# A two-layer diffusion trunk: values, queries and keys first, attention in half-tile steps beside four projections, residual loaded per token tile, first modulation in f32 by quarters

## The chip, the cores and the metric

The kernel runs on the 8 cores of one Trainium2 chip. Each core works on its own 1536 tokens and there is no traffic between cores. The metric is the time of the slowest core in microseconds (us).

An execution can fall into a second, slower state: the cores of one die (0 to 3 or 4 to 7), sometimes of both, get a lower TensorE clock, and the time grows whatever the kernel. Only fast runs are compared here. Where one die was slow I read the cores of the other, undisturbed die, and say so.

Engines in the profile lines: PE is TensorE, PEld its weight loads, DVE VectorE, ACT ScalarE, POOL GpSimd.

## The reference, cut to what matters

```python
# per layer, D = 2048, 4 branches of width 512; context tokens and latent tokens have their own modulation
m = silu(cond) @ w_ada + b_ada                  # shift1, scale1, gate1, shift2, scale2, gate2
h = rmsnorm(x, norm1_g) * (1 + sc1) + sh1
q, k, v, u, vg, xf, xp, gl = split(h @ w_in)    # 7 x 512 columns, then 4 x 2048 gate columns
branches = (attention(rmsnorm(q), rmsnorm(k), v),        # 8 heads of 64, neighbourhood + cached keys
            gelu(u) * (W_s @ rmsnorm(gelu(vg)) + b_s),   # gated branch
            fourier_mix(xf), multiscale_pool(xp))
merged = sum_i sigmoid(gl_i + b_i) * (branches[i] @ w_branch[i])
x = x + g1 * (merged @ w_out)
h2 = rmsnorm(x, norm2_g) * (1 + sc2) + sh2
x = x + g2 * (relu(h2 @ w_mlp1)**2 @ w_mlp2)
```

## The kernel before

A Python builder emits all instructions in order, per engine, with semaphores from a dependency tracker. The tokens of a core are three tiles of 512 (tile 0 is context, 1 and 2 are latent). A projection group is 16 matmuls of 512 columns into one PSUM bank. Weights come through a ring of 7 slots, cast to bf16 by POOL-issued transfers. Work of other engines is placed with `defer(n, fn)`: `fn` is emitted n hooks later. A hook comes after each group. Attention works in steps, or chunks (scores, exponentials and value products for a block or two of keys); a unit is all the steps of one head pair and one token tile, two of them for context and nine for a latent tile.

```python
    def hook(self):
        cur, self.deferred = self.deferred, []
        for d in cur:
            d[0] -= 1
        ...                                   # those at 0 are emitted, then the side generators step

    def gelu2(self, b, out, wk, i):
        g1, g2 = self.G1[i % 2], self.G2[i % 2]
        ps = self.bank(b)
        self.act(g1.ap(), ps, AF.Square, self.pk(b), [g1.k()])
        self.ts(g1.ap(), g1.ap(), 0.044715, 1.0, ALU.mult, ALU.add, [g1.k()], [g1.k()])
        self.tt(g2.ap(), g1.ap(), ps, ALU.mult, [g1.k(), self.pk(b)], [g2.k()])
        ...                                   # tanh on ACT, last operation on DVE

    # mixers: vg, u, values (gated branch as side work), q/k, then
        self.use_banks([0, 1], [])
        at = self.side(self.attention(l, BR, QP, QRt, KRt, QC, KX, V, VC), 1.0)
        ...                                   # xf, xp, Fourier, pool beside it

    # attention, at the end of a unit (one head pair, one token tile):
                self.act(self.RD.ap(), self.bank(DB), AF.Ln, self.pk(DB), [self.RD.k()], scale=2048.0)
                self.act(self.RD.ap(), self.RD.ap(), AF.Exp, [self.RD.k()], [self.RD.k()], scale=-1.0)
                self.tt(BR.ap(tt, j), self.bank(OB), self.RD.ap(), ALU.mult, ...)
    # and its loop, one step after each projection group:
        for i in range(0, len(chunks), 2):
            cur = chunks[i:i + 2]
            ...
            for ch in cur:
                scores(ch)
            for ch in prev:
                pv(ch)
            for ch in cur:
                probs(ch)
            prev = cur
            yield

    def out_proj(self, l, MRG, X, nrm):
        ...                                   # loads the residual of all three tiles
        def tile(slot, oc, tt):
            b = self.group(slot, MRG, tt, range(NCH))
            i = 0 if tt == 0 else 1
            self.stt(X.ap(tt, oc), self.bank(b), self.mv(l, 2, oc, i), X.ap(tt, oc), ALU.mult, ALU.add, ...)
            nrm.stat(tt, oc, 1)               # square on ACT now, ones-matmul one hook later
```

At the start all 32 tiles of the first modulation go through the ring in bf16, and after the last of them the norm of all three token tiles follows.

Of the kernel before, what the change touches and what calls it, by code (L numbers as in the profile page):

```python
# [13 lines left out]
NCH = 16  # L14
# [181 lines left out]

class Slot:
# [4 lines left out]
class Ring:  # L202


    def __init__(self, b, plan):
        self.b, self.plan = b, plan
        self.n = 0
        self.free = list(range(RING))
        self.home = []
        self.specs = []  # L210
        self.regs = [Reg(b.nc, b.base, f"W{i}", RING_OFF + i * SLOT, SLOT, BF16) for i in range(RING)]
# [29 lines left out]
class Builder:  # L241
    def __init__(self, plan=None):
        nc = bass.Bass("TRN2", target_bir_lowering=False)
        self.nc = nc
        self.decl_dram()
        base = nc.alloc_sbuf_tensor("POOL", [128, USABLE // 4], F32)
        self.base = nc_addr(base)
        self.tr = Tracker(nc)
        self.plan = plan
        self.alloc()  # L250
        self.ring = Ring(self, plan)
        self.deferred = []
        self.sides = []



    def decl_dram(self):
# [19 lines left out]
        self.d_cb = di("cb", (128, 768), BF16)  # L277
# [13 lines left out]
    def alloc(self):  # L291
# [10 lines left out]
        self.CB = const("CB", 768, BF16)  # L302
# [9 lines left out]
        self.PERM, self.FCC = cb(384, 512), cb(512, 768)  # L312
# [12 lines left out]
        self.ROPE = sreg("ROPE", 0, 8 * k, F32)  # L325
        self.G1 = [sreg(f"G1{i}", 8 * k + 4 * k * i, 2 * k, F32) for i in range(2)]
        self.G2 = [sreg(f"G2{i}", 10 * k + 4 * k * i, 2 * k, F32) for i in range(2)]
        self.QF = [sreg(f"QF{i}", 16 * k + 2 * k * i, 2 * k, F32) for i in range(2)]
        self.QR = [sreg(f"QR{i}", 20 * k + 2 * k * i, 2 * k, F32) for i in range(2)]
        self.QT = sreg("QT", 24 * k, 2 * k, F32)  # L330
        self.QS = [sreg(f"QS{i}", 26 * k + k * i, k, BF16) for i in range(2)]
        self.TAB = sreg("TAB", 0, 11776, F32)
        self.P = [sreg(f"P{i}", 11776 + 2048 * i, 2048, BF16) for i in range(3)]
        self.RD = sreg("RD", 11776 + 6144, 2048, F32)
        self.KC = sreg("KC", 11776 + 8192, 4096, BF16)
        self.PM = sreg("PM", 24064, 3200, BF16)
        self.WPB = sreg("WPB", 24064 + 3200, 1024, BF16)
# [30 lines left out]
    def hook(self):  # L368
# [3 lines left out]
        for d in cur:  # L372
            if d[0] <= 0:
                d[1]()
            else:
                self.deferred.append(d)
        for s in list(self.sides):
# [69 lines left out]

    def group(self, slot, src, tt, cs, lo=0):
# [3 lines left out]
        self.mms([(self.bank(b), slot.ap[:, lo + j * 128:lo + (j + 1) * 128], src.ap(tt, c), j == 0, j == n - 1)  # L452
                  for j, c in enumerate(cs)], r=[slot.keys, src.ks(tt, cs)], w=self.pk(b))
# [66 lines left out]
    class Norm:  # L520
# [23 lines left out]
        def apply(self, tt):  # L544
            b, l = self.b, self.l
# [3 lines left out]
            b.rsqrt(R.ap(), b.bank(bk), b.pk(bk), [R.k()])  # L549
            i = 0 if tt == 0 else 1  # L550
            for c in range(NCH):
                t = self.tmp['t'][c % len(self.tmp['t'])]
                b.stt(t.ap(), self.X.ap(tt, c), b.mod(l, i, self.which, c), R.ap(), ALU.mult, ALU.mult,
                      [self.X.k(tt, c), R.k(), b.MOD.k()], [t.k()])
                b.act(self.H.ap(tt, c), t.ap(), AF.Identity, [t.k(), b.MV.k()], [self.H.k(tt, c)],
                      bias=b.mv(l, 0 if self.which == 0 else 3, c, i), scale=1.0)
# [10 lines left out]
    def token_major(self, l, which, H, consume):  # L567
        slots = [self.ring.get(lambda b, kq=kq: b.d_tm[l, which, kq]) for kq in range(4)]
        for n in range(12):
            tt, q = divmod(n, 4)  # L570
            b = self.dbank()
            self.mms([(self.bank(b), H.ap(tt, c, q * 128, q * 128 + 128),
                       slots[c // 4].ap[:, (c % 4) * 512:(c % 4 + 1) * 512], c == 0, c == 15) for c in range(NCH)],
                     r=[s.keys for s in slots] + [H.ks(tt, range(NCH))], w=self.pk(b))
# [17 lines left out]
    def gelu2(self, b, out, wk, i):  # L592

        g1, g2 = self.G1[i % 2], self.G2[i % 2]
        ps = self.bank(b)
        self.act(g1.ap(), ps, AF.Square, self.pk(b), [g1.k()])
        self.ts(g1.ap(), g1.ap(), 0.044715, 1.0, ALU.mult, ALU.add, [g1.k()], [g1.k()])
        self.tt(g2.ap(), g1.ap(), ps, ALU.mult, [g1.k(), self.pk(b)], [g2.k()])
        self.act(g1.ap(), g2.ap(), AF.Tanh, [g2.k()], [g1.k()], scale=0.7978845608028654)
        self.stt(out, g1.ap(), 1.0, ps, ALU.add, ALU.mult, [g1.k(), self.pk(b)], [wk])  # L600

    def mixers(self, l, H, BR, WK, regs):
        tr = self.tr
        self.use_banks([0, 1, 2, 3], [4, 5, 6, 7])
        nm = lambda s: f"{s}_{l}"
        hreg, breg, wreg = regs
        brbase = breg.off

        BSB = self.reg(nm("BSB"), brbase + 8 * KB, 2 * KB, F32)
        GRW = self.reg(nm("GRW"), brbase + 10 * KB, 2 * KB, F32)  # L610
        WSB = self.reg(nm("WSB"), brbase + 12 * KB, KB, BF16)
        SSQ = self.reg(nm("SSQ"), brbase + 13 * KB, KB, BF16)
        SS = self.reg(nm("SS"), brbase + 14 * KB, 64, F32)
        NVS = [self.reg(nm(f"NVS{i}"), brbase + 24 * KB + 2 * KB * i, 2 * KB, F32) for i in range(2)]
        NKS = [self.reg(nm(f"NKS{i}"), brbase + 28 * KB + 2 * KB * i, 2 * KB, F32) for i in range(2)]
        VGT = [self.reg(nm(f"VG{n}"), brbase + (n // 4) * 16 * KB + (n % 4) * KB, KB, BF16) for n in range(12)]
        wo = wreg.off
        pair = lambda n, j, off, nb: self.reg(nm(f"{n}{j}"), wo + j * 8 * KB + off, nb, BF16)
# [5 lines left out]
        V = [self.reg(nm(f"V{n}"), wo + 32 * KB + n * KB, KB, BF16) for n in range(12)]  # L624
        VC = [self.reg(nm(f"VC{n}"), wo + 44 * KB + n * KB, KB, BF16) for n in range(4)]

        tr.dma('sp', lambda e: e.dma_start(out=BSB.ap(), in_=bass.AP(self.d_bs.tensor, l * 512, [[0, 128], [1, 512]])),
               w=[BSB.k()])
        tr.dma('sp', lambda e: e.dma_start(out=GRW.ap(), in_=bass.AP(self.d_gn.tensor, l * 512, [[0, 128], [1, 512]])),
               w=[GRW.k()])  # L630
        tr.dma('pool', lambda e: e.dma_start(out=WSB.ap(), in_=self.d_ws[l]), w=[WSB.k()])


        def vg_done(n, b):
            self.gelu2(b, VGT[n].ap(), VGT[n].k(), n)
            tr.op('act', lambda e: e.activation(out=SSQ.ap(), in_=VGT[n].ap(), func=AF.Square,
                                                accum_out=SS.ap(n, n + 1)),
                  r=[VGT[n].k()], w=[SSQ.k(), SS.k()])
        self.tables('exp_and_others')
        self.token_major(l, 0, H, vg_done)  # L640

        cnt = [0]
        for oc in range(4):
            def u_done(tt, b, oc=oc):
                self.gelu2(b, BR.ap(tt, 4 + oc), BR.k(tt, 4 + oc), cnt[0])
                cnt[0] += 1
            self.feature_major(l, 8 + oc, H, u_done)

        def gmlp():
            self.tables('natural_log_exp_and_others')  # L650
            self.rsqrt(SS.ap(0, 12), SS.ap(0, 12), [SS.k()], [SS.k()], scale=1.0 / BW, four=1)
            yield
            for n in range(12):
                self.stt(VGT[n].ap(), VGT[n].ap(), SS.ap(n, n + 1), GRW.ap(), ALU.mult, ALU.mult,
                         [VGT[n].k(), SS.k(), GRW.k()], [VGT[n].k()])
                tt, q = divmod(n, 4)
                b = self.abank()
                self.mms([(self.bank(b, g * 128, g * 128 + 128), VGT[n].ap(g * 128, g * 128 + 128),
                           WSB.ap(g * 128, g * 128 + 128), True, True) for g in range(4)],
                         r=[VGT[n].k(), WSB.k()], w=self.pk(b))  # L660
                t = self.QF[n % 2]
                self.tt(t.ap(), self.bank(b), BSB.ap(), ALU.add, [self.pk(b), BSB.k()], [t.k()])
                r, o = BR.loc(tt, 4)
                u = r.ap(o, o + 4 * TT).rearrange("p (g t) -> p g t", g=4)[:, :, q * 128:q * 128 + 128]
                keys = [r.k(o + g * TT + q * 128, o + g * TT + q * 128 + 128) for g in range(4)]
                self.stt(u, t.ap().rearrange("p (g t) -> p g t", g=4), 0.5, u, ALU.mult, ALU.mult,
                         [t.k()] + keys, keys)
                yield
        gs = self.side(gmlp(), 1.0)
# [8 lines left out]
        self.token_major(l, 1, H, v_done)  # L678
# [697 lines left out]
```

## Time and profile before

Four fast runs took 6255.7 to 6257.9 us, median 6257.2. The stage lines are in the prediction below. In short, for layer 0 of the slowest core:

| stage | us | what PE does in it |
|---|---|---|
| first modulation and norm, up to the first projection | about 181 | waits for transfers, then for the norm |
| all mixers, up to the merge | 709 (end) | waits on small statistics, on the cached keys, on the norm |
| merge | 857 | full |
| output projection | 300 | waits about 100 us for squares |
| MLP | 1411 | full |

How to read it: where PE is busy throughout at clock 1.00, nothing was expected from moving work about. What can be had lies in the other stages.

### The profile page before, as it was taken

Reading aid. Unit: us, or ns where it says so; the run is one execution under the profiler, and the core shown is the slowest. Engines: PE = TensorE matmul, PEld = TensorE weight load, DVE = VectorE, ACT = ScalarE, POOL = GpSimd, SP = SyncE. Lnnn points to the kernel's source line nnn. Section 1 sums busy time; section 2 is a strip of 40 time slices with the busy share of each in tenths; the row PEclk is TensorE's granted clock in tenths of the full one; section 3 lists DMA queues with packets and bytes.
Section 4 is the critical chain, followed back from the end, with each engine's and each line's share of the span. In section 5 each row is a group of like instructions: output and inputs, shape, how many; then the busy total and the mean of one; then the engine's idle time right before and its main releaser. Section 6 shows DMA issues by size and latency. Waiting matters only on the chain.

```text
span 6256.2 us, 73139 instructions; the slowest of 8 cores (6228.0 to 6256.2 us)
## 1 busy us (share of the span) xinstructions
PE 5727.5 (92%) x27208; PEld 2520.0 (40%) x27208; DVE 1899.5 (30%) x2721; ACT 1187.8 (19%) x1831; POOL 384.6 (6%) x732
## 2 busy tenths in 40 slices
PE   2788899999669999999998889999986899999999
PEld 0333344444224444444443334444432344444444
DVE  0543222222123222233344332222221333333333
ACT  1544211111121000000043451111111300000000
POOL 1000000100000000000000000000000000000000
PEclk6999899999999999999999999999999999999999
DMA  9232355553315555555343213322241222222223
GB/s 201 58 64 61 65 95 98 101 98 60 103 31 88 96 90 98 91 101 98 51 123 66 56 56 58 53 51 51 51 121 24 44 51 51 51 51 51 52 53 109
DMA packets 118728, 464.72 MB, mean 74 GB/s; under 512 B 13296, under 2 KB 15088, under 8 KB 109424
## 3 DMA queue, kind: packets, MB, share of 16 engines
q0 software_dynamic: 104704, 376.49, 34.5%
q1 hardware_dynamic: 13680, 83.56, 3.8%
q8 instruction: 226, 3.70, 0.2%
q14 instruction: 118, 0.97, 0.1%
HBM read 798.16 MB, written 29.36 MB: 132 GB/s over the span
## 4 chain that ended last, share of the span: by engine, by line
PE 87%; ACT 4%; DMA 4%; DVE 3%; issue 2%; ACTq 0%; DVEq 0%; SPq 0%; POOLq 0%
PE PS L425 87%; DMA W_96<-w_ada 2%; DVE x_B L418 1%; DMA SEL<-sel 1%; ACT bf_C L403 1%; DMA x_B<-xin 0%; DMA x_B<-xres 0%; DMA KC<-ckT 0%; DVE x_C L418 0%; ACT bf_A L403 0%; DVE x_A L418 0%; ACT G_62 L403 0%; ACT n_sq_11991 L403 0%; ACT n_sq_34868 L403 0%; ACT n_sq_11992 L403 0%
## 5 line engine op out<-in xcount | busy, mean ns | idle before, releaser
L418 DVE SCALAR_TENSOR_TENSOR x_B<-PS,MV,x_B 128x512 f32<-128x512 f32 x432 | 324.4, 751 | 581.6 <-PE PS L425 558.1
L403 ACT ACTIVATE RL_59<-PS 128x512 f32<-128x512 f32 x192 | 114.7, 597 | 1734.7 <-PE PS L425 1734.7
L425 PE MATMUL PS<-bf_A,W_99 128*128 128x512 bf16 x1344 | 299.4, 382 | 1.3 <-DVE VG_1_24334 L418 0.7
L412 DVE TENSOR_TENSOR HID<-RL_59 128x512 bf16<-128x512 f32 x192 | 133.1, 693 | 548.4 <-ACT RL_59 L403 548.4
L412 DVE TENSOR_TENSOR HID<-RL_60 128x512 bf16<-128x512 f32 x192 | 133.0, 693 | 538.2 <-ACT RL_60 L403 538.2
L425 PE MATMUL PS<-bf_A,W_93 128*128 128x512 bf16 x1296 | 293.8, 386 | 1.9 <-DVE bf_A L412 1.9
L425 PE MATMUL PS<-bf_C,W_95 128*128 128x512 bf16 x1296 | 291.0, 383 | 1.3 <-DVE VG_0_941 L418 0.7
L425 PE MATMUL PS<-bf_A,W_97 128*128 128x512 bf16 x1248 | 275.4, 379 | 0.0
L425 PE MATMUL PS<-bf_A,W_95 128*128 128x512 bf16 x1200 | 265.1, 379 | 0.0
L425 PE MATMUL PS<-bf_A,W_98 128*128 128x512 bf16 x1200 | 264.7, 379 | 0.0
L418 DVE SCALAR_TENSOR_TENSOR x_C<-PS,MV,x_C 128x512 f32<-128x512 f32 x216 | 162.2, 751 | 320.7 <-PE PS L425 312.7
L418 DVE SCALAR_TENSOR_TENSOR x_A<-PS,MV,x_A 128x512 f32<-128x512 f32 x216 | 162.2, 751 | 306.6 <-PE PS L425 299.7
L425 PE MATMUL PS<-bf_C,W_97 128*128 128x512 bf16 x1152 | 254.6, 379 | 0.0
L425 PE MATMUL PS<-bf_C,W_96 128*128 128x512 bf16 x1056 | 239.9, 386 | 8.6 <-ACT bf_C L403 8.6
L425 PE MATMUL PS<-bf_C,W_94 128*128 128x512 bf16 x1104 | 244.4, 379 | 2.0 <-DVE VG_0_938 L418 0.7
L425 PE MATMUL PS<-bf_C,W_99 128*128 128x512 bf16 x1056 | 237.2, 383 | 0.3 <-DVE bf_B L415 0.3
L425 PE MATMUL PS<-bf_C,W_98 128*128 128x512 bf16 x1008 | 224.9, 381 | 1.9 <-DVE bf_C L412 1.9
L418 DVE SCALAR_TENSOR_TENSOR TM_90<-TG_84,PS 128x512 f32<-128x512 f32 x64 | 44.0, 688 | 600.3 <-ACT TG_83 L403 496.1
L425 PE MATMUL PS<-bf_C,W_93 128*128 128x512 bf16 x1008 | 224.7, 381 | 0.0
L425 PE MATMUL PS<-HID,W_93 128*128 128x512 bf16 x1008 | 224.2, 379 | 0.0
L403 ACT ACTIVATE RL_60<-PS 128x512 f32<-128x512 f32 x192 | 114.7, 597 | 550.8 <-PE PS L425 550.8
L425 PE MATMUL PS<-HID,W_96 128*128 128x512 bf16 x912 | 202.0, 379 | 0.0
(990 smaller groups left out, 7331.5 us busy)
## 6 DMA issues: line engine op xcount, KB each, us to landing
W_94<-w_m POOLq DMA_DIRECT2D x38, 512.0 KB, 6.1
W_93<-w_m POOLq DMA_DIRECT2D x38, 512.0 KB, 6.2
W_96<-w_m POOLq DMA_DIRECT2D x37, 512.0 KB, 6.2
W_97<-w_m POOLq DMA_DIRECT2D x37, 512.0 KB, 6.1
W_99<-w_m POOLq DMA_DIRECT2D x36, 512.0 KB, 6.1
W_95<-w_m POOLq DMA_DIRECT2D x36, 512.0 KB, 6.1
W_98<-w_m POOLq DMA_DIRECT2D x34, 512.0 KB, 6.2
W_93<-w_ada POOLq DMA_DIRECT2D x31, 512.0 KB, 6.6
```

The lines of the kernel that those rows point to most:

```text
L403: self.tr.op('act', lambda e: e.activation(out=out, in_=in_, func=func, **kw), r=r, w=w)
L412: self.tr.op('dve', lambda e: e.tensor_tensor(out, a, b, op), r=r, w=w)
L418: self.tr.op('dve', lambda e: e.scalar_tensor_tensor(out, a, s, b, op0, op1), r=r, w=w)
L425: ins = e.matmul(out, lt, rh, start=st, stop=sp, skip_group_check=True)
```

## The change

Intent: let PE find dense work in the stages where it waited. Cut to its core:

```diff
-    def hook(self):
+    def tick(self):
         ...
+        if self.attn is not None and next(self.attn, 'end') == 'end':
+            self.attn = None
+
+    def hook(self):
+        self.tick()
         ...
+    def chain(self, lst, r, w):
+        n = len(lst) // 2
+        if self.attn is None:
+            self.mms(lst, r, w)
+        else:
+            self.mms(lst[:n], r, w)
+            self.tick()
+            self.mms(lst[n:], r, w)
 ...                                          # mixers: values, q/k, then attention with vg, xf, u, xp
-            self.defer(1, rest)
+            self.defer(2, rest)
 ...
+        def gelu2(b, n, last):
+            x, g = G[n % 2]
+            self.copy('act', x.ap(), self.bank(b), self.pk(b), [x.k()])
+            self.stt(g.ap(), x.ap(), 0.044715, x.ap(), ALU.mult, ALU.mult, [x.k()], [g.k()])
+            self.stt(g.ap(), g.ap(), 1.0, x.ap(), ALU.add, ALU.mult, [x.k(), g.k()], [g.k()])
+            self.defer(2, lambda: self.act(g.ap(), g.ap(), AF.Tanh, [g.k()], [g.k()], scale=0.7978845608028654))
+            self.defer(3, lambda: last(x, g))
 ...                                          # attention
+        def divide(j, tt, lo):
+            d = self.DC.ap(lo, lo + 128)
+            k = self.DC.k(lo, lo + 128)
+            tr.op('dve', lambda e: e.reciprocal(d, d), r=[k], w=[k])
+            self.tt(BR.ap(tt, j, lo, lo + 128), self.OC.ap(lo, lo + 128), d, ALU.mult, ...)
 ...                                          # end of a unit, in place of Ln, Exp and multiply
+                while state['div']:
+                    state['div'].pop(0)()
+                self.copy('act', self.DC.ap(), self.bank(DB), self.pk(DB), [self.DC.k()])
+                self.copy('dve', self.OC.ap(), self.bank(OB), self.pk(OB), [self.OC.k()])
+                for lo in range(0, TT, 128):
+                    state['div'].append(lambda lo=lo: divide(j, tt, lo))
 ...
+        for i, ch in enumerate(chunks):
+            scores(ch)
+            if i >= 2:
+                pv(chunks[i - 2])
+            probs(ch)
+            if state['div']:
+                state['div'].pop(0)()
             yield
 ...                                          # out_proj; four square buffers instead of two
-            nrm.stat(tt, oc, 1)
+            nrm.stat(tt, oc, 2)
 ...                                          # start, for tile m of the 32 of the first modulation, in f32
+            self.mms(lst, r=[reg.k(), ZF.k()], w=self.pk(bank))
+            load(m + 4)
 ...
+            if m % 8 < 7:
+                continue
+            self.copy('dve', stage.ap(), self.bank(bank), self.pk(bank), [stage.k()])
 ...                                          # selector matmuls, four DVE operations
+            for c in range(nb * 4, nb * 4 + 4):
+                norm.chunk(0, c)
+            cs = range(nb * 4, nb * 4 + 4)
+            for n in range(4):
+                self.mms(self.tm_list(n, slots, H, n, cs), [slots[nb].keys, H.ks(0, cs)], self.pk(n))
```

The residual is laid out by token tile, and a tile is loaded right after its part of the last merge channel. Fourier and pool follow alone on all 8 banks. The landing tiles of the first modulation take 1 MB each, four of them.

## The prediction

> **What bounds the kernel now.** I read the page first, then the core list (all eight granted 0.973 to 0.977, spans 6228 to 6256 us: an undisturbed run), then the busy time by stage, then the chain and PE's waits inside the stages where PE is not full.
>
> ```profile
> PE 5727.5 (92%) x27208; PEld 2520.0 (40%) x27208; DVE 1899.5 (30%) x2721; ACT 1187.8 (19%) x1831; POOL 384.6 (6%) x732
> PE 87%; ACT 4%; DMA 4%; DVE 3%; issue 2%; ACTq 0%; DVEq 0%; SPq 0%; POOLq 0%
> ```
>
> PE is the bound. It can't do its matmuls faster here, so a gain has to come from stages in which it waits. By stage (span, PE, weight load, DVE, ACT, POOL busy, granted clock, DMA share, GB/s):
>
> ```profile
> 41.00:151.04 110.04, 26.77 (x140) 5.84 (x141) 0.69 (x1) 10.97 (x19) 16.76 (x32) 0.55 1.00 202
> 151.04:246.79 95.75, 59.73 (x232) 23.71 (x233) 49.04 (x79) 67.36 (x117) 0.76 (x3) 0.83 0.22 39
> 343.62:461.80 118.18, 97.11 (x424) 41.05 (x424) 49.74 (x72) 57.85 (x91) 4.75 (x9) 0.99 0.34 63
> 461.80:590.00 128.20, 117.21 (x691) 48.34 (x691) 41.04 (x54) 50.72 (x60) 2.65 (x5) 0.96 0.20 58
> 709.10:1566.00 856.90, 856.87 (x4097) 378.06 (x4098) 218.70 (x335) 133.03 (x193) 75.48 (x143) 1.00 0.51 90
> 1566.00:1866.00 300.00, 198.22 (x849) 82.91 (x848) 66.33 (x93) 55.82 (x86) 8.97 (x17) 0.97 0.29 67
> ```
>
> These are the first modulation, norm with the first projection, queries and keys, half of attention, merge, and output projection of layer 0. Merge (and the MLP, 1391 of 1411 us) is full: nothing to win. The output projection idles a third of its time. Why, in the order of time and in the waits of that stretch:
>
> ```profile
> 1839.97 0.38 PE L425 MATMUL PS<-n_sq_11991,CB 128*128 128x512 bf16 x1 [1.85 <-ACT n_sq_11991 L403]
> 1840.18 3.61 PE L425 MATMUL PS<-bf_A,W_98 128*128 128x512 bf16 x16
> 1845.86 0.38 PE L425 MATMUL PS<-n_sq_11992,CB 128*128 128x512 bf16 x1 [2.06 <-ACT n_sq_11992 L403]
> 1846.08 5.30 PE L425 MATMUL PS<-bf_A,W_93 128*128 128x512 bf16 x16
> ```
>
> ```profile
> PE PS L425 <- ACT n_sq_11991 L403: 48.9, 24, 6.2
> PE PS L425 <- ACT n_sq_11992 L403: 47.7, 24, 4.9
> ```
>
> After each of 48 tiles PE waits about 1.85 us for the residual add and the square of the tile it has just made; after some waits the next 16 matmuls take 5.30 instead of 3.61 us, a lowered clock. Two long DMA pieces of the chain, and PE's waits in the queries and keys and at the start:
>
> ```profile
> 459.62 12.40 DMA KC<-ckT
> 1568.88 27.31 DMA x_B<-xin
> ```
>
> ```profile
> 372.00 0.38 PE L425 MATMUL PS<-QS_71,CB 128*128 128x512 bf16 x1 [0.62 <-ACT QS_71 L403]
> 372.22 3.61 PE L425 MATMUL PS<-bf_C,W_97 128*128 128x512 bf16 x16
> 376.78 0.38 PE L425 MATMUL PS<-QS_72,CB 128*128 128x512 bf16 x1 [0.95 <-ACT QS_72 L403]
> ```
>
> ```profile
> 143.26 0.62 PE L425 MATMUL PS<-W_94,Z 128*32 128x512 bf16 x4 [5.29 <-DMA W_94<-w_ada]
> 181.41 1.87 PE L425 MATMUL PS<-W_97,bf_C 128*128 128x512 bf16 x4 [12.80 <-ACT bf_C L403]
> 212.08 1.87 PE L425 MATMUL PS<-W_97,bf_C 128*128 128x512 bf16 x4 [15.40 <-DVE VG_0_930 L418]
> ```
>
> The start is a DMA stage (share 1.00) until 151 us, followed by a latency stage until 247 us.
>
> **What the Trainium skill says.** "TensorE: Matmul & The Clock Gate", Part 1: 512 columns start every 215.7 ns warm, 426.7 ns cold, and idling makes it cold. Agrees: 16-matmul groups of the merge follow each other in 3.45 us (0.216 each), and the granted clock reads 0.50 through the DMA stage. "DMA: Bandwidth & Descriptors", Specifications: about 358 GB/s of HBM per core. Agrees nearly: plain f32 loads alone moved 339 to 348 GB/s (1582 to 1597 us). "FP8 and Floating Point Precision", TensorE Precision Notes: true f32 takes four passes. No f32 matmul of this width is in the trace. "VectorE: DVE Perf Modes", walkthrough of the 8-slice pipeline: reciprocal repeats its divide step 8 times. No row shows one yet.
>
> **Output projection (both layers).** The norm statistic is now put two ticks behind instead of one, so a whole group (3.45 us) runs while DVE (0.75) and ACT (0.63) prepare it; needed is about 1.85. Four square buffers instead of two keep ACT from waiting. The residual is laid out so that a token tile covers only its own third of the two dying regions, and the last merge channel runs tile by tile: tile 0's load starts some 35 us before the projection, tile 2's at its start but is wanted about 11 us later by DVE and 18 us later by PE. At 340 GB/s its first 1 MB needs about 3 us, so I take it as hidden. New stage: 48 x (3.45+0.22) = 176, plus the 3.3 us wait at the head of the MLP that is not touched, plus 5 chosen = 184. Before: 300 and 305. **Gain 116+121 = 237.**
>
> **Mixers.** PE work of one layer, by columns: 84 groups of 16 = 290; queries' and keys' small matmuls 40 x 0.216 = 9; spatial mixing 3; attention 28,416 columns per head pair at 2.4 per ns = 47; Fourier 36; pool 6: 391. Before, layer 1 took 3277 to 3788 = 511, layer 0 from 181 to 709 = 528. New:
> - values: 12 x 3.45 = 41, one plain copy per group, plus 2 at the border = 43;
> - queries, keys: 24 x 3.45+9 = 92, statistic one group later (the 0.6 to 1.0 us waits go), 5 for the flush of the last chain: 97. Before 118;
> - the cached keys, bias table and values load at the start of this stage, in regions of their own: the 12.4 us wait goes;
> - attention with four projections: 48 groups in halves make 96 steps for 82 attention steps. 48 x 3.45 = 166, attention 47, spatial 3, and a mode change per step (pairs of steps before cost about 0.2 us beyond their columns) 16: 232. Beside it per group of about 5 us: ACT 2 exps of 1.02, copy 0.60, tanh 0.63, square 0.8 = 4.1; DVE up to 2 bias adds of 1.22 and 3 or 4 ops of 0.7 = 4.6 to 5.2. DVE is just full in local steps, half idle in the others, so I add 10 for lateness: 242. The reciprocals (estimate from the skill: 128 x 8 cycles = 1.1 us) fall in steps without bias by construction;
> - Fourier and pool alone, on 8 banks: 36+6 PE, 6 for the last Fourier weights (this wait stays: ring depth is the same), about 15 for evictions and short matmuls: 63.
>
> Sum 445 against 511: **gain 66 in layer 1**.
>
> **Start (layer 0).** Bytes before the last modulation tile: residual 12.6 MB, modulation 33.5, value weights 4.2, constants 0.4 = 50.7 MB; at 340 GB/s 149 us, plus 3 to begin, 2 to land and 4 for quarter borders, at which PE holds the landing slots about 13 us with some 12 us of loads in flight: T = 158 (before 149.5). The f32 matmuls: four side by side, as bf16 ones are (0.62 us for 4 cold), at four passes 1.7 us cold per tile against 3.1 us of DMA: hidden. After T: eviction, selection, modulation 5; four norm chunks and 16 value matmuls 9; then tiles 1 and 2 of the values 28, and about 5 behind the norm of tile 2 on ACT: values end near 205. Then 97+242+63: merge starts near 607 instead of 709. **Gain 102.**
>
> **Rest.** The last MLP chunk of layer 0 (106 us for 48 x 1.94 = 93 of PE) gets a later statistic: gain 8. Merge does the same matmuls: 0. Total 102+116+8+66+121 = 413: 6257-413 = 5844. I add 11 for what I can't see: **5855**.
>
> **Rivals.** (1) DVE becomes the bound of the half-tile steps: two banks only for the projections, and in-order queues in which a bias add waits behind GELU ops. For: 5.2 us of DVE against 5 in local steps. Against: over the stage DVE sums to about 190 of 242 us even with slow reciprocals. Would cost up to 0.5 us a step, 40 per layer: about 5935. (2) f32 matmuls of four column strips don't overlap: 6.8 us per tile cold, 3.4 warm: the start turns PE-bound and ends 40 us or more later: about 5900. (3) The residual load turns into a new wait in the output projection, as its 12.6 MB still need 37 us while weights come: at most 15 per layer, 5885. (4) Nearly no lateness: attention at 232, Fourier and pool at 52, start at 150: about 5800. (5) Denser PE lowers the granted clock: merge and MLP are at 0.99 to 1.00 while full, which speaks against.
>
> **Range and chances.** The output projection is the surest term (measured waits, ample slack): 237 +-15. The mixers 66+60 have +-25 per layer, the start +-20. Independent: about +-45; rivals weigh to the slow side. Range 5790 to 5935. Even with the output projection alone it would be 3.8% faster: faster 0.97, within 2% 0.02, slower 0.01.
>
> **What would show it.** Right: output projection tiles 3.7 us apart with no wait on a square, about 184 us; no chain piece on the residual or cached keys; queries and keys about 97; attention stage about 242; modulation finished near 158 with DMA share 1.00 throughout; merge starting near 607. Wrong, if PE shows waits on probabilities or on GELU copies in nearly every step, if DMA share falls under 0.9 between 40 and 155 us, if statistics still wait, or if the merge grows beyond 857 us.

## The result, and the profile after

The changed kernel took 5980.0 to 5984.8 us in four fast runs, median 5981.4, against 6257.2. Executions in which one die ran at a lower clock are left out of the means. The ratio of the fast runs is 0.956 (95% interval 0.9544 to 0.9577): faster by 4.4%. (A ratio is the mean time of one kernel's fast runs over that of the other's fast runs of the same rounds, so not quite the ratio of the medians.) The predicted time was 5855, the range 5790 to 5935: the direction was right and the result lies above the range. Of the expected 402 us, 276 came.

Engines over the whole run, from the page of the changed kernel:

```profile
PE 5682.6 (95%) x26823; PEld 2508.8 (42%) x27360; DVE 2017.4 (34%) x2932; ACT 1165.6 (19%) x1809; POOL 367.7 (6%) x700
```

PE is at 95% of a shorter span instead of 92%. Busy times by stage on its slowest core, columns as in the prediction (stretch, length, PE, PEld, DVE, ACT, POOL, granted clock, DMA share, GB/s). They are first modulation, queries and keys, attention with projections, output projection, all in layer 0:

```profile
37.30:186.50 149.20, 74.42 (x355) 19.20 (x361) 20.92 (x40) 36.27 (x60) 0.00 (x0) 0.71 0.80 268
229.25:331.80 102.55, 94.31 (x417) 40.80 (x425) 46.41 (x69) 58.41 (x94) 9.51 (x18) 0.98 0.48 84
331.80:632.00 300.20, 254.85 (x1367) 96.66 (x1393) 186.80 (x280) 122.78 (x180) 6.34 (x12) 0.95 0.15 37
1546.30:1729.20 182.90, 178.89 (x817) 81.29 (x833) 60.68 (x85) 55.80 (x86) 8.97 (x17) 1.00 0.41 81
```

The last line is the success: 182.9 us against 300.0, clock 1.00. The tiles in the order of time show no wait any more:

```profile
1714.64 0.38 PE L440 MATMUL PS<-n_sq_12078,CB 128*128 128x512 bf16 x1
1714.86 3.62 PE L440 MATMUL PS<-bf_A,W_88 128*128 128x512 bf16 x16
```

The first line is one failure: the modulation's DMA share is 0.80, not 1.00, so it ends at 186.5 us instead of 158. The third is the larger one: attention takes 300 us, of which PE is busy 255 and idle 45. Against the prediction, layer 0 and layer 1:

| step | predicted | measured |
|---|---|---|
| values end (layer 0) | 205 | 229.3 |
| queries and keys | 97 | 102.6, 102.7 |
| attention with projections | 242 | 300.2, 298.5 |
| Fourier and pool | 63 | 56.0, 55.8 |
| merge starts (layer 0) | 607 | 688.0 |
| output projection to the MLP, layer 0 | 184 | 182.9 |

The misses are +24, 2 x +5.6, +58 and +57, 2 x -7: together about +136. Less the 11 us that the prediction added for the unseen this is 125, and the miss is 126. So two places have to be explained: the attention stage and the start.

Who PE waited for in the attention stage of layer 0 (core 3, from its first scores to about the end of the projections; columns: total us, times, longest us):

```profile
PE PS L440 <- DVE OC L424: 13.6, 7, 3.7
PE PS L440 <- DVE bf_B L433: 11.1, 4, 5.4
PE PS L440 <- ACT P_62 L418: 4.9, 3, 2.5
```

`OC` is the copy of the attention output out of PSUM, `bf_B` the gated branch's data, `P` the exponentials. None of them is in every step, as the prediction had feared; they are few and long. One such wait in the order of time (core 2), the PE line first and then what DVE did in that time:

```profile
412.44 0.64 PE L440 MATMUL PS<-P_63,VC_0_963 128*64 128x512 bf16 x2 [3.29 <-DVE OC L424]
```

```profile
406.89 0.69 DVE L433 SCALAR_TENSOR_TENSOR G_0_948<-G_0_947 128x512 f32<-128x512 f32 x1 [0.87 <-ACT G_0_947 L422]
407.69 0.69 DVE L433 SCALAR_TENSOR_TENSOR G_0_948<-G_0_948,G_0_947 128x512 f32<-128x512 f32 x1
408.30 0.68 DVE L433 SCALAR_TENSOR_TENSOR bf_B<-G_0_946,G_0_945 128x512 bf16<-128x512 f32 x1
408.90 0.94 DVE L853 RECIPROCAL DC<-DC 128x128 f32<-128x128 f32 x1
...
410.16 0.95 DVE L853 RECIPROCAL DC<-DC 128x128 f32<-128x128 f32 x1
...
411.60 0.69 DVE L424 COPY OC<-PS 128x512 f32<-128x512 f32 x1
```

The output was ready in PSUM at about 407. The copy that frees its bank starts at 411.60, behind gelu operations and two divides left over from the unit before. PE can't begin the next unit, and at its restart eight matmuls take 2.92 us instead of 1.90: the granted clock was 0.56 between 412.4 and 416.

Two things are at work in this wait. One is order: before 406.89 DVE idles 0.87 us for ACT's gelu copy, although the inputs of the divides behind it had been copied by 403.5. The other is a buffer: there is one `OC` and one `DC` (the denominators), so neither copy may start, on whatever engine, before the divides of the unit before have read them. ACT, which copies `DC`, stands idle for that:

```profile
411.59 0.59 ACT L422 COPY DC<-PS 128x512 f32<-128x512 f32 x1 [4.80 <-DVE bf_B L427]
```

A context unit has only two steps, and the four divides are taken one per step. So this comes at the three context units that follow another unit, with PE waits of 3.29, 0.99 and 4.14 us: 8.4 of the 14.8 us that core 2 waits for `OC`. No run gave the copies a second pair of buffers.

### The profile page after: what moved, and what is told of

Its sections match the earlier page's. It is cut to its first block, busy times and chain, and to the rows that moved or that the text cites. A ratio compares the mean times of both kernels' runs of the same rounds, so it can differ in the third digit from the quotient of the medians.

```text
span 5980.1 us, 72984 instructions; the slowest of 8 cores (5963.0 to 5980.1 us)
## 1 busy us (share of the span) xinstructions
PE 5682.6 (95%) x26823; PEld 2508.8 (42%) x27360; DVE 2017.4 (34%) x2932; ACT 1165.6 (19%) x1809; POOL 367.7 (6%) x700
## 4 chain that ended last, share of the span: by engine, by line
PE 89%; DVE 3%; ACT 3%; issue 2%; DMA 2%; SPq 0%; DVEq 0%; ACTq 0%; POOLq 0%
PE PS L440 89%; DMA LT_124<-w_ada 2%; DVE PS L433 1%; ACT bf_C L418 1%; DVE DC L853 0%; ACT bf_A L418 0%; DVE G_0_948 L433 0%; DVE bf_B L433 0%; DVE G_0_946 L433 0%; DVE G_1_24384 L433 0%; DVE OC L424 0%; DVE G_1_24382 L433 0%; ACT P_62 L418 0%; DVE bf_B L427 0%; SPq L1240 0%
## 5 line engine op out<-in xcount | busy, mean ns | idle before, releaser
L440 PE MATMUL PS<-bf_A,W_87 128*128 128x512 bf16 x1269 | 287.8, 382 | 2.4 <-DVE bf_B L424 0.9
L440 PE MATMUL PS<-bf_A,W_86 128*128 128x512 bf16 x1270 | 286.6, 381 | 1.5 <-issue 0.2
L440 PE MATMUL PS<-bf_A,W_85 128*128 128x512 bf16 x1173 | 266.4, 382 | 1.7 <-issue 0.5
L440 PE MATMUL PS<-bf_A,W_88 128*128 128x512 bf16 x1176 | 263.9, 379 | 1.4 <-issue 0.2
L440 PE MATMUL PS<-bf_A,W_90 128*128 128x512 bf16 x1128 | 253.0, 379 | 1.5 <-issue 0.3
L440 PE MATMUL PS<-HID,W_88 128*128 128x512 bf16 x987 | 222.4, 380 | 1.4 <-issue 0.3
L440 PE MATMUL PS<-bf_A,W_91 128*128 128x512 bf16 x890 | 203.2, 381 | 2.9 <-DVE bf_B L430 1.4
```

Of the source, the lines that this page charges most:

```text
L440: ins = e.matmul(out, lt, rh, start=st, stop=sp, skip_group_check=True)
```

## The experiments

Stage times below are read from the traces as medians over the cores named. "Attention to pool" is from the first score matmul to the last pool matmul; it includes Fourier and pool, starts 3.5 us into the stage, and is 348.8 us in layer 0 and 347.4 in layer 1 of the changed kernel. "Core span" is the median span of the cores: 5973.4 for the changed kernel. Theory A for the attention stage: DVE and ACT take their work in order, and short attention work stands behind gelu work and divides. Rivals: the amount of DVE work; the changes of matmul shape; the half-tile steps themselves; and, tried by no run, the single pair of buffers `OC` and `DC`.

### e1_old_start: what is the new start worth?

```diff
-first = self.start(X, H)       # f32 by quarters
+old start: modulation in bf16 through the ring, norm of all tiles, then values first
```

> The changed kernel with the start of the kernel before: first modulation cast to bf16 through the weight slots, all three token tiles normed after it, then values first as in the changed kernel. Theory (the new start is worth little, because its transfers stop at each quarter border): values end near 238 us instead of 229, whole kernel +5 to +15 us on 5981. Rival (the new start carries a good part of the gain as the prediction had it, 205 against 238): +25 us or more. If it is faster than 5981, the new start costs time outright.

Correct; three fast runs of 5993.9, 6018.6 and 6020.1. In the latter two one die ran at a clock of 0.975 against 0.980. The profiled run had all cores alike, median span 5988.7. The first statistic of the queries (two groups after the values' end) comes at 245.7 us instead of 233.2, everything after it takes as long as in the changed kernel. So the new start is worth 12.5 us there, 15 on the span, where the prediction's 205 for the values' end, against the 238 that I estimated for an old start with values first, makes 33. The 238 was right (245.7 less the two groups of 3.6). Theory held.

### e2_stat_delay1: where does the output projection's gain come from?

```diff
-            nrm.stat(tt, oc, 2)
+            nrm.stat(tt, oc, 1)
```

> The changed kernel with one number put back: the statistic matmul of the out projection follows its tile after one step instead of two (the four square buffers and the earlier residual loads stay). Theory (the gain of that stage is the delay): out projection back from 183 to about 300 us in each layer, waits of 2 to 2.5 us on the scalar engine's squares in most of the 48 tiles, total near 6200. Rival (the gain came from the residual loads): it stays under 200 us, total under 6015.

Correct; fast run 6175.6. From first to last statistic the stage takes 266.7 and 272.2 us in the two layers instead of 172.8; before it was 282.6 and 280.6. PE's waits in the stage of layer 0 (slowest core):

```profile
PE PS L440 <- ACT n_sq L418: 88.0, 48, 1.9
```

One wait of 1.83 us for each of the 48 tiles is back. The single number carries about 193 us of the two layers' gain. The rest, 8 to 16 us per layer, is left to the residual loads and the extra buffers, which were not tried apart. The theory's direction and most of its size held. The stage stayed under the 300 us because this run kept those other two parts.

### e3_oc_on_act: is it the engine that copies?

```diff
-self.copy('dve', self.OC.ap(), self.bank(OB), ...)
+self.copy('act', self.OC.ap(), self.bank(OB), ...)
```

> The changed kernel with the copy of the attention output out of PSUM (12 per layer) on the scalar engine instead of the vector engine. Theory (the matmuls wait for a vector engine that is late): the 14.8 us of waits on that copy go, attention stage 300 to about 285-290, total 15 to 30 us less. Rival (the wait moves to the scalar engine, which takes everything in order too): the waits on that copy fall but waits on the exponentials grow by as much, total within 8 us of 5981.

Correct; fast runs 6001.0 and 6021.9, in both of which one die was slower than the other; on the better die (0 in the profiled run, clock 0.984) attention to pool takes 345.2 and 344.9, core span 5967.5. That is 3 us per layer. The waits of core 1 in that stage:

```profile
PE PS L440 <- ACT P L418: 13.4, 9, 2.5
PE PS L440 <- ACT OC L422: 12.7, 5, 5.5
```

The wait moved along with the copy, so another engine for it is not enough. But the run can't tell order from buffers. The three longest of these five waits (4.43, 1.36 and 5.53 us, 11.3 of 12.7) are those of the context units, where ACT idles until DVE's divides have read the old `DC` and `OC`, as here:

```profile
409.76 0.59 ACT L422 COPY DC<-PS 128x512 f32<-128x512 f32 x1 [4.80 <-DVE bf_B L427]
410.25 0.59 ACT L422 COPY OC<-PS 128x512 f32<-128x512 f32 x1
```

So the rival, that ACT is late because it takes everything in order, is not shown by them.

### e4_no_reciprocal: is it the amount of DVE work?

```diff
-tr.op('dve', lambda e: e.reciprocal(d, d), ...)
-self.tt(BR, OC, d, ALU.mult)
+self.stt(BR, OC, 2e-6, d, ALU.mult, ALU.mult)      # wrong on purpose
```

> Wrong result on purpose: the 48 reciprocals of a layer's attention are left out and the divide is one multiply by the denominator and a constant. Takes 45 us of the vector engine's 187 us in the stage. Theory (lateness of the in-order vector engine makes the stage 300 instead of 242): stage falls to 260-270, total 60 to 80 us less. Rival (the change of matmul shape twice per half tile and the unhidden attention matmuls make it): stage stays over 290, total less by under 20 us.

Wrong result, as meant; fast runs 5953.8 and 5953.8. Attention to pool 335.2 and 333.4, core span 5947.1. DVE lost 45 us of work per layer and the stage lost 14: between both expectations. The amount matters, but three quarters of the excess remain. The waits left, on core 1:

```profile
PE PS L440 <- ACT P L418: 11.6, 9, 2.1
PE PS L440 <- DVE bf_B L433: 9.1, 4, 5.4
PE PS L440 <- DVE OC L424: 8.8, 5, 2.6
```

### e5_border_later: why did the transfers stop at the start?

```diff
 self.mms(lst, ...)                 # modulation tile m
 load(m + 4)
-if m % 8 == 7: copy, selector matmuls, norm of 4 blocks, 16 value matmuls
+if m % 8 == 7: copy
+if m % 8 == 1 and m > 8: selector matmuls, norm of 4 blocks of the quarter before
+if m % 8 == 3 and m > 8: 16 value matmuls of the quarter before
 (m == 31: the last quarter's own work, as before)
```

> The changed kernel with the work at the three inner quarter borders of the first modulation moved behind later weight tiles: the selector matmul and the norm of four columns come one and two tiles into the next quarter, the 16 value matmuls four tiles into it. Theory (the tensor engine stands at each border for 13 to 16 us and so keeps the four landing tiles full, and the transfers stop): the DMA share no longer falls to 0 at the inner borders, the modulation ends 20 to 27 us earlier (near 160 instead of 175-185 us), total 15 to 25 us less than 5981. Rival (the memory rate bounds the start, the stops only shift waiting): the modulation's end moves by under 8 us.

Correct; fast runs 5965.6, 5967.9 and one of 6024.8 with a slower die. First the windows of 5 us round the first quarter border in the changed kernel, then the same in this run (core 5; the last two figures are DMA share and GB/s):

```profile
70.00:75.00 5.00, 5.00 (x17) 1.77 (x19) 0.00 (x0) 0.00 (x0) 0.00 (x0) 0.58 0.00 0
75.00:80.00 5.00, 3.49 (x32) 0.79 (x25) 0.00 (x0) 0.00 (x0) 0.00 (x0) 1.00 0.39 131
```

```profile
70.00:75.00 5.00, 4.37 (x15) 1.02 (x8) 1.35 (x3) 2.17 (x4) 0.00 (x0) 1.00 1.00 347
75.00:80.00 5.00, 3.51 (x19) 0.99 (x16) 0.00 (x0) 2.19 (x4) 0.00 (x0) 1.00 1.01 341
```

A share of 0.00 means that all four landing tiles were full and PE, in order, stood at the border's work and did not empty them. With that work moved, the share stays near 1 until 150 us and the modulation ends at 162.5 us (cores 4 and 5) instead of 181.3. The queries' first statistic moves from 233.2 to 218.2. The two clean runs are 13 to 16 us shorter. Theory held at its lower edge: the end of the modulation moves by 19 us, but 4 of them are lost again to the norm of the last tile behind it (PE's wait for ACT before the last values is 6.1 us on core 5, against 3.0 on core 2 of the changed kernel).

### e6_gmlp_earlier: the gated branch

```diff
     self.rsqrt(self.SS ...)
+    yield
-    for n in range(13): scale block n; if n: small matmuls of block n - 1
+    for n in range(14): scale block n; if n > 1: small matmuls of block n - 2
-gs = self.side(gmlp(), 1.34)
+gs = self.side(gmlp(), 1.5)
```

> The changed kernel with one empty step between the gated branch's reciprocal root and its first scaling, and its small matmuls two steps behind the scaling instead of one. Theory: the 11.4 us of matmul waits on the scaled block in each layer go, attention stage 10 to 12 us shorter in each layer, total 20 to 24 us less. Rival (the scalar engine's table switch delays the exponentials anyway): the wait on the scaled block turns into a wait on the exponentials, total within 8 us of 5981.

Correct; one fast run, 5973.9 (-8). Attention to pool 344.2 and 343.6: 4 us per layer, not 11. A later trace (e11, core 1) shows why:

```profile
393.69 0.79 PE L440 MATMUL PS<-WSB,bf_B 128*128 128x128 bf16 x8
...
398.57 3.57 PE L440 MATMUL PS<-bf_C,W 128*128 128x512 bf16 x8 [4.09 <-DVE bf_B L433]
```

The small matmuls (first line) take turns with the projections on the same two PSUM banks, and the next projection half (second line) waits until DVE has emptied the bank of the gated branch. In e6's own trace (core 3) the waits before the small matmuls are gone too, and 10.1 us of waits on `bf_B` remain, now before projection halves. The scaling that I had made earlier was only one part of that wait.

### e7_whole_groups: the half-tile steps themselves

```diff
 chain: self.mms(lst, r, w)                        # not cut in two
 hook:  self.tick()
+       if self.attn is not None: self.tick()      # two chunks after a whole group
```

> The changed kernel with attention steps in pairs between whole projection groups instead of one step after each half group; everything else as it is. Theory (late vector and scalar engines make the stage): fewer places where a chunk's work is hidden, so more waits, stage from 300 to 310 or more in each layer. Rival (the change between matmul shapes costs much, here halved for the projections): one return to full shape saved per pair, 40 x 0.1 us, and the stage falls, at most by 4 us per layer plus what the longer undisturbed groups give.

Correct; a single fast run, 6053.0, in which die 1 was slower. On die 0 attention to pool takes 351.9 and 350.2, 3 us per layer more than with half tiles. The first scores also come 2 us later after the first statistic (101.4 us instead of 99.1), and the core span is 5981.9, 8.5 us longer. The direction is the theory's, but the size is small: the half-tile steps, the idea in the title, are worth 3 to 5 us per layer in this order of work.

### e8_attention_first: only the order

```diff
 def tick(self):
+    attention chunk (scores, value products, copies, bias add, exponential, divide)
     deferred work (gelu's tanh and last operations)
-    attention chunk
 def gelu2(...):
-    two DVE operations at once
+    self.defer(1, the two DVE operations)         # so they too come behind the chunk
```

> The changed kernel with another order of the same instructions: in each half step the attention chunk's vector and scalar work goes ahead of the delayed gelu work, and the two first gelu operations of the vector engine are delayed behind it. Theory (the matmuls wait because short attention work stands in line behind gelu work on two engines that wait for each other): waits on the output copy and the exponentials fall from 27 us to 15 or less, stage 10 to 15 us shorter in each layer, total 20 to 30 us less. Rival (it is the amount of work on the vector engine, not the order): within 5 us per layer, total within 10 us of 5981.

Correct; one fast run, 5939.7, 42 us under the changed kernel. Attention to pool on die 0 is 327.2 and 326.5: 21 us per layer, more than expected. Waits of core 3, to be held against the three lines of the same core above:

```profile
PE PS L440 <- DVE bf_B L433: 11.1, 4, 5.4
PE PS L440 <- DVE OC L424: 8.5, 4, 2.9
PE PS L440 <- ACT P L418: 1.1, 3, 0.7
```

The waits on exponentials (10.9 us over the three buffers before) are nearly gone and those on the copy fell from 13.6 to 8.5. DVE's busy time in the stage is the same, 184 against 185 us. Taking away 45 us of its work had given 14 us; taking away nothing and changing the order gives 21. Of the 8.5 us left on the copy, 5.9 (2.03, 0.99 and 2.92) are those of the context units, where the buffers are taken. The two edits of this run were not tried apart.

### e9_three_together, e10_two_divides, e11_two_flushes, e12_all_edits: do the parts add, and what is left?

```diff
 e9:  e5 + e6 + e8
 e10: e9, and
-     if state['div']: state['div'].pop(0)()
+     for _ in range(min(2, len(state['div']))): state['div'].pop(0)()
 e11: e10, and
-     self.flush()                       # after q/k: PE waits for the last statistics
+     attention starts one vg group later, the last statistics run beside two vg groups
+     start: half of the norm of tile 2 spread behind value groups
 e12: e11, and in each gated step
+     small matmuls of block n - 2 and their eviction
      scale block n
-     small matmuls of block n - 2 and their eviction
```

> The changed kernel with three of the edits together: border work of the first modulation later, the gated branch's root one step earlier, attention's short work ahead of the gelu work. Alone they took about 15, 8 and 43 us off. Theory (three separate waits): the gains add, 60 to 80 us less than 5981 (5900 to 5920), more than the sum if the gated branch's wait of 11 us a layer now lies open. Rival (they shorten the same wait): under 50 us less.

> The kernel with the three edits, and two quarters of the softmax divide in each step instead of one, so that no divide is left over when the next short context unit ends and none falls into a step with a bias. Theory (what is left of the wait on the output copy, 8 to 9 us a layer, is the copy standing behind left-over divides): that wait goes, attention stage 6 to 9 us shorter in each layer. Rival (two divides make 2.5 us of vector work in one step of 2.7 us): other waits of the same size appear, stage within 3 us.

> The kernel with the three edits and two divides a step, and two drains covered: the last query and key statistics run beside the first two value-gate groups (the 6.8 us of waits at the end of the query and key stage), and half of the norm of the last token tile at the start is spread behind value groups (wait of 6.1 us). Theory: query and key stage 6 to 8 us shorter in each layer and the values at the start done 3 to 6 us earlier, 15 to 22 us less than the same kernel without. Rival (the waits turn up again at the first attention chunks): under 6 us less.

> All edits so far together (border work later, gated branch's root earlier, attention's short work first, two divides a step, the two covered drains), and in each gated step the vector engine empties the shared projection bank before it scales the next block. This is the version meant to beat both. Expected from the undisturbed cores of the run before it (5876 to 5890 us) less 0 to 8 us for the bank: 5870 to 5890 us, about 1.5 per cent under 5981 and 6 per cent under the kernel before. Rival for the last edit (the bank waits because the divides stand in front of both operations): 5880 to 5890, the waits on that bank unchanged at 7 us a layer.

All four are correct. Median core spans, undisturbed die or run, against 5973.4:

| run | core span | attention to pool | read from |
|---|---|---|---|
| e9 | 5909.2 | 323.0, 323.2 | die 1 of a slow run; no fast run |
| e10 | 5910.8 | 324.1, 322.7 | all cores; fast run 5915.8 |
| e11 | 5883.8 | 315.4, 314.2 | die 0 of a slow run; no fast run |
| e12 | 5879.3 | 313.6, 311.9 | die 1 of a slow run; one fast run, 5887.5 |

e9: 64 us, against 13, 8 and 39 on the core spans of the single runs (5960.2, 5965.7, 5934.3): they add. Two divides per step (e10) changed nothing. But the run did not clear the copy's way: in its trace (core 5) two of the four divides still run right before the copy of a context unit (at 380.06 and 381.32, the copy at 382.77), since four divides take 5 us and such a unit two steps of 2.7. So it doesn't settle whether these divides hold the copy up. Covering the two drains (e11) took 27 us off. From the first statistic to the first score went from 99 to 95 us, although one more group of 3.6 us now lies in it, and attention to pool from 323 to 315, partly because that group left it. The sum of both fell by 12 to 13 us per layer, more than the 6.8 us of waits that were meant; waits on the copy fell as well, from 8.4 us (e10, core 5) to 3.1 (e11, core 1). The edit at the start shows no gain: the first statistic comes at 217.3 us instead of 217.6 (die 0). The last edit (e12) took 4 to 5 us. Against the changed kernel's 5981.4, measured in other rounds, e12's one fast run is 94 us shorter, or 1.6%; the fast runs of the kernel before in e12's own rounds are 6255.5, 6256.3, 6261.6 and 6309.5. So it beats both, though with one fast run there is no interval.

## Why the prediction was wrong

**Output projection: right.** Predicted 184, measured 182.9, and e2 shows that the named cause (a statistic one step too early) carries most of it. The MLP of layer 0 took 1402.3 against 1403, the merge 858.3 against 857, at a clock of 1.00: rivals 3 (a new wait on the residual) and 5 (a lower clock) fell.

**Attention with projections: the sum had the right parts and two were too small.** The step that failed is "so I add 10 for lateness: 242", together with "a mode change per step ... 16". Lateness first: the stretch of 300.2 us has 45 idle, of which 10 were allowed. What the prediction called rival 1, at up to 40 us a layer, is what came about. It was weighed down with the argument that DVE sums to about 190 of 242 us. That sum was right (187), and it was the wrong test. e4 and e8 show why: 45 us less DVE work gives 14, another order of the same work gives 21. "PSUM — Partial Sum Buffer" of the Trainium skill, section "Engine vs sequencer instructions", says that the queues of ScalarE and VectorE are strictly first in, first out. The trace agrees: DVE idles 0.87 us for a gelu copy with divides ready behind it, and the copy that PE waited 3.29 us for starts only after the gelu work and divides emitted before it. Moreover ACT's copy for the gelu stood behind exponentials that waited for DVE, and DVE's gelu behind ACT's copy, so each engine's lateness was handed to the other: in the stage of layer 0 (core 2) DVE waited 44 us in all for ACT's gelu copies, and ACT's exponentials 88 us for DVE's bias adds. In e8 (core 3) these are 3.7 and 55 us. Part of the lateness is not order alone: 8.4 us of the waits on the copy in this stage come where the only buffer pair is still being read.

Then the shape changes. A step without any wait, from the changed kernel (core 2):

```profile
562.47 0.39 PE L440 MATMUL PS<-QR_0_974,KR_0_978 64*128 64x512 bf16 x2
562.79 0.41 PE L440 MATMUL PS<-P_63,VC_0_965 128*64 128x512 bf16 x2
563.03 0.38 PE L440 MATMUL PS<-P_63,CB 128*64 128x512 bf16 x2
563.34 1.90 PE L440 MATMUL PS<-bf_C,W_87 128*128 128x512 bf16 x8
```

A 512-column matmul takes 0.216 us, and I take the same for a pair on two halves of the array. From start to start the lines take 0.32, 0.24 and 0.31, and the eight matmuls before 562.47, which start at 560.64, take 1.83 instead of 1.73. The value products and the denominators share a shape and follow each other in 0.24; the three changes of shape come to about 0.10 us each. In e7 (core 1) a whole group of 16 takes 3.55 us up to the next scores instead of 3.45, so the 0.10 comes once per change and not per matmul. The step takes 2.70 us, with 0.3 for changes where I had put 0.2: some 8 to 10 us per layer over 82 steps. The rest of the 23 us by which PE's busy time exceeds the predicted 232 goes with the lower clock, 0.95, after waits. I didn't measure that part by itself.

"The reciprocals fall in steps without bias by construction" was also wrong: the changed kernel pops one quarter per step, so some meet bias adds. With the other edits in place this cost nothing that shows: e10, where none should meet one, took as long as e9.

**Start: the mechanism was right, the term for the borders was too small.** The failing step is "4 for quarter borders, at which PE holds the landing slots about 13 us with some 12 us of loads in flight". PE did hold them for 13 to 16 us, but the transfers stopped for 8 to 10 us at each of three borders (5-us windows with a share of 0.00 to 0.77, as the two shown under e5), about 27 us where the term had 4. The modulation ended 28 us late on the slowest core, 23 on the median of the cores. When PE turned to the first border at 60.8 (core 2), the loads in flight lasted until 70.4, so 9.6 us and not 12. The queue could issue no more until PE freed a tile at 76.0, and that load landed 7.7 us after its issue. e5 gives back 19 us. The f32 matmuls were as hidden as predicted: about 1.1 us warm and 1.9 cold per tile of 1 MB, so rival 2 fell.

**Queries and keys: "5 for the flush of the last chain" was 8.7** (323.08 to 331.79). The two waits, at the end of the stage on core 2:

```profile
327.01 0.59 PE L440 MATMUL PS<-QS_0_937,CB 128*128 128x512 bf16 x1 [3.55 <-ACT QS_0_937 L422]
331.30 0.59 PE L440 MATMUL PS<-QS_0_938,CB 128*128 128x512 bf16 x1 [3.28 <-ACT QS_0_938 L422]
```

e11 shows that they can be covered by other groups.

**Fourier and pool: 7 us better than said**; the margin for evictions was too large. Besides the wait on the last Fourier weights, 6.0 us as predicted, PE waited 2.6 us there.

What stays open: nobody tried a second `OC` and `DC`, though up to 8.4 us of PE's waits in layer 0 hang on the single pair; the two edits of e8 were not separated, and the part of the attention stage that is due to a lower clock after each wait was not isolated. The waits on the banks shared with the gated branch remain in the best version.

## What to carry to other kernels

When two engines feed each other through queues that run in order, a busy share of 60% says little. Ask for each short operation that PE needs what stands ahead of it in its queue, and emit the operations that PE needs first. Ask also whether its buffers are free by then: where they were not, another engine for it did not help (e3). Before work is put at a border of a pipelined load, ask how long the consumer stands there against what the landing buffers hold. A statistic that trails its tile needs the whole chain of two other engines as slack; one number in an emitter was worth 193 us here.

## What the Trainium skill lacked or had wrong

- "TensorEngine Tiling (Array Packing)", Key Properties, says that changing the tiling mode drains TensorE and gives no cost. Here a change cost about 0.10 us between full-array, row-tiled and column-tiled matmuls, three times per step, and 0.02 between two column-tiled pairs. Whether the drain is what takes the time, the traces don't show.
- "VectorE: DVE Perf Modes" gives the repeat of 8 for the reciprocal but no duration. My estimate from it was 1.1 us for 128 f32 columns; the 48 reciprocals of a layer took 0.946 us each.
- "FP8 and Floating Point Precision" gives four passes for f32 and doesn't say whether column strips still overlap. Four strips of 512 f32 columns took 1.06 us warm together, against 0.86 for four passes of 0.216 us and 3.45 if the strips followed one another: they overlap.
- I found no page that says what the order of emission on in-order engines can cost: 21 us per layer of 349 here, with the same instructions.
